# A hybrid layer on one core: fewer idle turns in a reordered opening, a context bank emptied by two copies, one weight and some row scalings moved back

## The chip, the core and the metric

The kernel runs on one core of a Trainium2 chip. A core has five engines that run side by side, each with its own queue of instructions in a fixed order: TensorE (PE in the profile: matrix products, its weight loads PEld), VectorE (DVE), ScalarE (ACT), GpSimd (POOL) and SyncE (SP), which here only issues the transfers from memory. They wait for each other by semaphores. Data live in memory (HBM), in SBUF (128 partitions) and in PSUM, whose banks of 128 x 512 floats take the results of TensorE. The metric is the device time of one execution in microseconds (us), lower is better.

## The reference

One layer of a diffusion backbone, for 1024 latent tokens on a 64-wide grid and 256 context tokens, with 1024 channels, in fp32. Cut to what matters:

```python
sh1, sc1, g1, sh2, sc2, g2 = jnp.split(c_silu @ w_ada[l] + b_ada[l], 6, axis=-1)
hx = _modulate(_rmsnorm(x, norm1_g[l]), sh1, sc1)      # h * (1 + scale) + shift
hc = _modulate(_rmsnorm(ctx, norm1_g[l]), csh1, csc1)
(xq, xk, xv, xrq, xrk, xrv, xrg, xga, xgb) = jnp.split(hx @ w_in[l], IN_OFFSETS, axis=-1)
...
o_na = _na_latent(...)      # neighbourhood attention, 8 heads of 64, plus all context keys
o_ret_x, _, _ = _bi_retention(...)   # 4 heads, keys of 128, values of 256, chunks of 128
o_ret = _ret_output(o_ret_x, xrg)
x = x + g1 * _merge(o_na, o_ret, xga, xgb, w_proj_na[l], w_proj_ret[l], w_out[l])
hx2 = _modulate(_rmsnorm(x, norm2_g[l]), sh2, sc2)
x = x + g2 * _conv_ffn(hx2, w_up[l], conv_w[l], conv_b[l], w_down[l])
...
return _rmsnorm(x, final_norm_g)
```

`_merge` multiplies the attention's output by `w_proj_na` (`w_pna` in the kernel) and the retention's by `w_proj_ret`, weighs each with a sigmoid gate and projects the sum by `w_out`. The first retention states come from the context tokens.

## The kernel before

Each fp32 operand is split into a rounded high part (a cast on ScalarE, line 89) and the remainder (a subtraction on VectorE, line 90). A product is then three TensorE products, high x high, high x low, low x high (`mm3`, lines 113 to 115; 124 to 126 when it is called through other helpers). Tokens come in tiles of 128 (`tb` 0 to 7 latent, 8 and 9 context), channels in eight blocks of 128 (`kb`).

The work runs in stages: the opening to about 92 us, attention to about 370, retention to about 700, then the attention's projection `pn` with its gates, the retention's projection and the output projection to about 1130, the up-projection to 1500, the down-projection to the end. Outside two hand-ordered blocks a scheduler sets each engine's order from estimated costs; instructions that are marked `late` may be put back.

*The opening* (from line 652) is ordered by hand: the lines of that block are the order on each engine. `load_x` and `load_ag` load token tiles and pieces of the modulation weight on SP; `load_f` loads the first attention weight. `square_x` (ScalarE), `rstd_x` (GpSimd), `scale_x` (VectorE) normalise a tile; `transp` turns its blocks on TensorE into PSUM (line 207). `ag_mm` (283) multiplies a piece of the modulation weight by the conditioning columns, `ag_ev`, `ag_tr` (293) and `ag_fin` make per-channel scale and shift of it, and `mod_h`, `mod_v`, `mod_l` make the high part, the full value and the low part of the modulated block. `evac_t` moves a turned block out of PSUM first. `first_mm(half, kb)` is the first attention pair's projection: nine products per block; `next_mm` the second pair's. `ctx_h`, `ctx_v`, `ctx_l` and `ctx_mm` do the same for the context tokens. `turn_idle` (197) lets TensorE transpose the identity for nothing; here 83 times.

*Retention.* `front(i)` projects one token tile of a head to queries, keys and values in one PSUM bank. For a context tile (`i < NCB`) three readers follow: the cast of the values (1138), the subtraction for their low part (1139), the copy of the keys `r0` (1143).

*Attention's projection.* After retention eight tiles `onr` of the attention's output are loaded and turned into banks `tpn` (1371; the pool `g` holds six banks), and split into `ona` (1373 on ScalarE, 1374 on VectorE). `hx_sums(k)` makes four sums of gate operands: GpSimd adds high and low parts into four buffers `b` (1354, from the pool `r` of ten, which also holds the `onr` tiles), VectorE combines them (1357) in four operations. `wpn` are the first two weights of the projection `pn`.

*The end of the down-projection.* For the last column half of token rows 4 to 7, VectorE forms a row part, GpSimd multiplies it by the gate (1972) and adds the residual (1973), ScalarE squares it (1923), and `early_part` (1927, 1928, GpSimd) scales it by the final gain.

Of the kernel before, what the change touches and what calls it, by code (L numbers as in the profile page):

```python
# [8 lines left out]
F32 = mybir.dt.float32  # L9
# [31 lines left out]
def tile_hybrid_layer(ctx, tc: tile.TileContext, io, dbg=None):  # L41
# [610 lines left out]
    with tc.manual_schedule():  # L652
        make_sel()
        load_x(0)
        square_x(0)
        load_x(3)
        load_x(2)
        load_cc()
        rstd_x(0, 1)
        load_x(1)  # L660
        square_x(3)
        scale_x(0)
        load_ag(0, 0)
        transp(0, (3,), ("c0",), idle=34)
        transp(0, (6,), ("c1",))
        load_ag(0, 1)
        silu_cc()
        load_cols()
        square_x(2)
        ag_mm(0, 0, idle=24)  # L670
        rstd_x(3, 1)
        load_ag(1, 0)
        transp(0, (7,), ("tp",))
        square_x(1)
        ag_mm(0, 1)
        transp(0, (0,), ("c1",), idle=3)
        load_ag(1, 1)
        transp(0, (5,), ("c1",))
        scale_x(3)
        transp(3, (6,), ("c1",))  # L680
        load_f(0, 0)
        rstd_x(2, 1)
        transp(3, (0,), ("c1",))
        scale_x(2)
        transp(0, (4,), ("c0",))
        rstd_x(1, 1)
        ag_ev(0, "act")
        transp(2, (3,), ("c0",))
        transp(3, (5,), ("c1",), idle=4)
        ag_tr(0)  # L690
        load_ag(2, 0)
        scale_x(1)
        load_ag(2, 1)
        load_f(0, 1)
        transp(2, (0,), ("c1",))
        transp(3, (3,), ("c0",))
        transp(2, (7,), ("tp",))
        one_plus()
        transp(1, (0,), ("c1",))
        transp(1, (6,), ("c1",))  # L700
        ag_mm(1, 0, idle=5)
        transp(1, (5,), ("c1",))
        ag_mm(1, 1)
        transp(0, (1,), ("c0",))
        load_ag(4, 0)
        transp(2, (4,), ("c0",))
        ag_fin(0)
        transp(1, (7,), ("tp",))
        mod_h(True, 0, 0)
        ag_ev(1, "act")  # L710
        load_f(0, 2)
        transp(2, (1,), ("c0",))
        transp(0, (2,), ("c1",))
        transp(1, (3,), ("c0",))
        load_x(5)
        transp(3, (1,), ("c0",))
        transp(2, (6,), ("c1",))
        mod_v(True, 0, 0)
        load_x(4)
        load_x(6)  # L720
        transp(3, (4,), ("c0",))
        transp(3, (7,), ("tp",))
        transp(2, (2,), ("c1",))
        mod_l(True, 0, 0)
        transp(1, (1,), ("c0",), idle=4)
        split_hi(0, 0)
        evac_t(True, 0, 3, "vec")
        ag_tr(1)
        ag_mm(2, 0, idle=5)
        load_x(7)  # L730
        evac_t(True, 0, 7, "act")
        ag_fin(1)
        mod_v(True, 0, 1)
        mod_h(True, 0, 1)
        ag_mm(2, 1)
        transp(1, (4,), ("c0",))
        transp(3, (2,), ("c1",))
        transp(2, (5,), ("c1",))
        split_lo(0, 0)
        ag_ev(2, "act")  # L740
        evac_t(True, 0, 4, "vec")
        load_ag(3, 0)
        transp(1, (2,), ("c1",), idle=4)
        split_hi(0, 1)
        ag_tr(2)
        split_hi(0, 2)
        ag_mm(4, 0)
        load_ag(3, 1)
        split_lo(0, 1)
        ag_fin(2)  # L750
        load_ag(4, 1)
        split_lo(0, 2)
        mod_l(True, 0, 1)
        load_ag(4, 2)
        mod_h(True, 0, 2)
        load_ag(4, 3)
        evac_t(True, 0, 6, "vec")
        mod_v(True, 0, 2)
        square_x(5)
        first_mm(0, 0)  # L760
        rstd_x(5, 1)
        mod_l(True, 0, 2)
        square_x(4)
        rstd_x(4, 1)
        square_x(6)
        scale_x(4)
        load_ex()
        first_mm(0, 1)
        scale_x(5)
        load_ag(5, 0)  # L770
        rstd_x(6, 1)
        scale_x(6)
        first_mm(0, 2)
        transp(4, (3,), ("c1",))
        ag_mm(3, 0)
        square_x(7)
        load_x(8)
        transp(4, (2,), ("c1",))
        load_x(9)
        rstd_x(7, 1)  # L780
        transp(5, (2,), ("c1",))
        transp(4, (0,), ("c1",))
        scale_x(7)
        transp(6, (3,), ("c1",))
        next_load(0)
        ag_mm(3, 1)
        transp(6, (2,), ("c1",))
        transp(6, (0,), ("c1",))
        evac_t(True, 0, 5, "act")
        transp(7, (2,), ("c1",))  # L790
        load_ag(5, 1)
        transp(7, (0,), ("c1",))
        transp(5, (3,), ("c1",))
        transp(7, (3,), ("c1",))
        ag_ev(3, "vec")
        transp(5, (0,), ("c1",))
        ag_tr(3)
        ag_mm(4, 1)
        transp(4, (5,), ("c1",))
        transp(4, (7,), ("c1",))  # L800
        transp(7, (5,), ("c1",))
        transp(6, (7,), ("c1",))
        evac_t(True, 1, 2, "vec")
        transp(6, (5,), ("c1",))
        transp(4, (4,), ("tp",))
        ag_fin(3)
        transp(5, (7,), ("c1",))
        transp(5, (5,), ("c1",))
        evac_t(True, 1, 0, "act")
        ag_mm(4, 2)  # L810
        transp(7, (4,), ("tp",))
        mod_h(True, 1, 0)
        ag_mm(4, 3)
        transp(4, (6,), ("c1",))
        mod_h(True, 0, 3)
        transp(5, (4,), ("tp",))
        transp(5, (6,), ("c1",))
        load_f(1, 0)
        mod_v(True, 1, 2)
        transp(6, (6,), ("c1",))  # L820
        load_f(1, 2)
        transp(6, (4,), ("tp",))
        transp(7, (7,), ("c1",))
        mod_v(True, 0, 3)
        mod_l(True, 0, 3)
        mod_v(True, 1, 0)
        ag_ev(4, "vec")
        evac_t(True, 1, 5, "act")
        transp(7, (6,), ("c1",))
        mod_h(True, 1, 2)  # L830
        first_mm(0, 3)
        transp(4, (1,), ("tp",))
        evac_t(True, 1, 3, "act")
        mod_v(True, 1, 3)
        transp(6, (1,), ("tp",))
        ag_tr(4)
        mod_l(True, 1, 0)
        evac_t(True, 1, 6, "vec")
        ag_fin(4)
        evac_t(True, 1, 7, "act")  # L840
        mod_v(True, 0, 4)
        transp(5, (1,), ("tp",))
        mod_l(True, 1, 2)
        evac_t(True, 1, 4, "act")
        transp(7, (1,), ("tp",))
        first_mm(1, 0)
        square_x(8)
        mod_v(True, 1, 1)
        mod_h(True, 1, 3)
        square_x(9)  # L850
        mod_h(True, 0, 4)
        load_ag(5, 2)
        first_mm(1, 2)
        mod_h(True, 1, 1)
        rstd_x(9, 1)
        mod_l(True, 0, 4)
        ag_mm(5, 0)
        mod_h(True, 1, 4)
        ag_mm(5, 1)
        ag_mm(5, 2)  # L860
        load_ag(5, 3)
        split_hi(1, 0)
        ag_mm(5, 3)
        mod_l(True, 1, 1)
        mod_h(True, 0, 5)
        scale_x(9)
        load_f(1, 1)
        mod_v(True, 1, 4)
        rstd_x(8, 1)
        first_mm(1, 1)  # L870
        mod_l(True, 1, 4)
        ag_ev(5, "act")
        split_lo(1, 0)
        mod_h(True, 1, 5)
        ag_tr(5)
        split_hi(1, 2)
        next_load(1)
        mod_l(True, 1, 3)
        scale_x(8)
        split_lo(1, 2)  # L880
        transp(8, (4,), ("tp",))
        split_hi(1, 1)
        mod_v(True, 1, 5)
        mod_l(True, 1, 5)
        ag_fin(5)
        first_mm(1, 3)
        split_lo(1, 1)
        transp(8, (2,), ("tp",))
        transp(9, (3,), ("tp",))
        transp(9, (5,), ("tp",))  # L890
        transp(9, (4,), ("tp",))
        mod_v(True, 0, 7)
        mod_h(True, 1, 7)
        mod_v(True, 0, 6)
        transp(8, (3,), ("tp",))
        ctx_h(3)
        first_mm(1, 4)
        mod_h(True, 1, 6)
        next_hi(0)
        mod_v(True, 1, 6)  # L900
        mod_h(True, 0, 6)
        transp(9, (2,), ("tp",))
        transp(8, (5,), ("tp",))
        ctx_v(3)
        mod_l(True, 1, 6)
        mod_v(True, 0, 5)
        load_bc()
        ctx_v(2)
        first_mm(0, 4)
        transp(8, (6,), ("tp",))  # L910
        mod_l(True, 0, 6)
        first_mm(1, 6)
        transp(8, (0,), ("tp",))
        ctx_h(2)
        ctx_h(5)
        mod_h(True, 0, 7)
        ctx_l(2)
        first_mm(1, 5)
        ctx_v(4)
        first_mm(0, 6)  # L920
        transp(9, (0,), ("tp",))
        ctx_l(3)
        ctx_h(4)
        ctx_v(5)
        mod_l(True, 0, 5)
        transp(9, (6,), ("tp",))
        ctx_h(6)
        ctx_l(4)
        mod_v(True, 1, 7)
        mod_l(True, 0, 7)  # L930
        first_mm(0, 5)
        ctx_v(6)
        ctx_h(0)
        ctx_l(6)
        transp(9, (1,), ("tp",))
        transp(8, (1,), ("tp",))
        ctx_v(1)
        next_lo(0)
        first_mm(0, 7)
        transp(9, (7,), ("tp",))  # L940
        ctx_h(1)
        mod_l(True, 1, 7)
        ctx_l(5)
        transp(8, (7,), ("tp",))
        first_mm(1, 7)
        ctx_v(0)
        ctx_l(1)
        ctx_l(0)
        ctx_v(7)
        ctx_h(7)  # L950
        ctx_l(7)
        s0.release()
# [18 lines left out]
        next_hi(1)  # L971
        ev_hi(1, 1, 0)
        next_lo(1)
        ev_hi(2, 1, 0)
        ev_hi(0, 1, 1)
        ev_lo(0, 1, 1)
# [1142 lines left out]
```

## Time and profile before

| | us |
|---|---|
| median of 3 runs (lowest, highest) | 1734.16 (1733.9, 1735.04) |
| the profiled execution | 1735.01 |
| its span, first to last instruction | 1733.2 |
| TensorE busy | 1717.1 (99%) |
| VectorE, ScalarE, GpSimd busy | 1222.2, 839.6, 540.4 |
| mean granted TensorE clock | 0.998 |

The page of the profile gives busy time by engine, the chain of work that ended last, and groups of instructions by line. A row of the timeline is: start, length of the group, engine, line, operation, output<-inputs, shapes, count, and in brackets the idle time before it with what ended it. A row of the windows is: stretch, its length, then busy time and count for PE, PEld, DVE, ACT and POOL, the granted clock, the busy share of the transfer engines and GB/s. Products overlap, so a group's length runs past the start of the next.

### The profile page before, as it was taken

Reading aid. Unit: us, or ns where it says so; the run is one execution under the profiler, and the core shown is the slowest. Engines: PE = TensorE matmul, PEld = TensorE weight load, DVE = VectorE, ACT = ScalarE, POOL = GpSimd, SP = SyncE. Lnnn points to the kernel's source line nnn. Section 1 sums busy time; section 2 is a strip of 40 time slices with the busy share of each in tenths; the row PEclk is TensorE's granted clock in tenths of the full one; section 3 lists DMA queues with packets and bytes.
Section 4 is the critical chain, followed back from the end, with each engine's and each line's share of the span. In section 5 each row is a group of like instructions: output and inputs, shape, how many; then the busy total and the mean of one; then the engine's idle time right before and its main releaser. Section 6 shows DMA issues by size and latency. Waiting matters only on the chain.

```text
span 1733.2 us, 25367 instructions
## 1 busy us (share of the span) xinstructions
PE 1717.1 (99%) x8552; PEld 1435.8 (83%) x8552; DVE 1222.2 (71%) x2461; ACT 839.6 (48%) x1796; POOL 540.4 (31%) x706
## 2 busy tenths in 40 slices
PE   9999999999999999999999999999999999999997
PEld 7788888888888888888888888788788888888886
DVE  5778787665676766855555657867888889856756
ACT  6566666563453434543444333644444444545444
POOL 2100000002334343512223121012667667311444
PEclk9999999999999999999999999999999999999999
DMA  9344455532231223588975656768666776998744
GB/s 378 95 138 143 141 158 160 151 118 64 68 101 37 77 46 109 180 273 256 277 241 201 217 184 181 272 216 230 172 165 179 196 192 168 261 313 294 242 153 175
DMA packets 142002, 313.04 MB, mean 181 GB/s; under 512 B 19152, under 2 KB 32112, under 8 KB 135664
## 3 DMA queue, kind: packets, MB, share of 16 engines
q1 hardware_dynamic: 117536, 230.40, 38.6%
q0 software_dynamic: 12032, 70.27, 18.1%
q10 hardware_dynamic: 12304, 10.75, 1.8%
q8 instruction: 67, 1.10, 0.2%
q14 instruction: 63, 0.52, 0.1%
HBM read 250.78 MB, written 121.91 MB: 215 GB/s over the span
## 4 chain that ended last, share of the span: by engine, by line
PE 81%; issue 5%; DMA 5%; DVE 5%; POOL 2%; ACT 2%; SPq 0%; POOLq 0%; ACTq 0%; DVEq 0%
PE u L1379 28%; PE mm L126 4%; PE mm L124 4%; PE mm L125 4%; PE mm L115 4%; PE mm L114 4%; PE mm L113 4%; PE y L1379 2%; PE R L516 2%; DMA ur<-d_a 2%; PE pr L114 2%; PE pr L113 2%; PE pr L115 2%; PE ptp L498 2%; PE om L125 1%
## 5 line engine op out<-in xcount | busy, mean ns | idle before, releaser
L1379 PE MATMUL u<-T,wc 128*128 128x512 f32 x960 | 225.3, 390 | 0.7 <-ACT pu L1413 0.5
L1379 PEld LDWEIGHTS u<-T,wc 128*128 128x128 f32 x960 | 179.4, 188 | 40.9 <-ACT pu L1413 3.7
L1379 PE MATMUL y<-wc,ahl 128*128 128x512 f32 x924 | 210.1, 389 | 0.4 <-DVE wc L90 0.4
L1379 PEld LDWEIGHTS y<-wc,ahl 128*128 128x128 f32 x924 | 173.3, 188 | 36.8 <-DVE wc L90 0.8
L90 DVE TENSOR_TENSOR wc<-ur,wc 128x512 fp32r<-128x512 f32 x161 | 119.2, 743 | 62.6 <-ACT wc L89 60.8
L89 ACT CAST wc<-ur 128x512 fp32r<-128x512 f32 x161 | 99.7, 621 | 117.7 <-PE u L1379 74.1
L114 PE MATMUL mm<-low,wc 128*128 128x512 f32 (+1 forms) x312 | 118.9, 381 | 0.0
L1379 PE MATMUL u<-h2a,wc 128*128 128x512 f32 x480 | 113.1, 390 | 0.4 <-DVE pu L1422 0.4
L113 PE MATMUL mm<-hx,wc 128*128 128x512 f32 x264 | 107.4, 407 | 0.3 <-ACT hc L227 0.3
L1379 PEld LDWEIGHTS u<-h2a,wc 128*128 128x128 f32 x480 | 89.7, 188 | 20.5 <-issue 1.5
L115 PE MATMUL mm<-hx,wc 128*128 128x512 f32 x264 | 105.3, 399 | 0.0
L1379 PE MATMUL u<-hxT,wc 128*128 128x512 f32 x384 | 89.6, 389 | 0.0
L587 POOL COPY pad<-pu 128x1 f32<-128x1 f32 x54 | 36.6, 678 | 163.2 <-DVE pu L1416 120.9
L587 POOL COPY pad<-st 128x1 f32<-128x1 f32 x32 | 5.9, 185 | 257.7 <-DVE st L490 257.7
L1379 PEld LDWEIGHTS u<-hxT,wc 128*128 128x128 f32 x384 | 72.1, 188 | 14.9
L89 ACT CAST wc<-raw 128x512 fp32r<-128x512 f32 x86 | 53.1, 621 | 43.6 <-PE pr L115 9.2
L126 PE MATMUL mm<-wc,low 128*128 128x512 f32 (+1 forms) x180 | 68.9, 383 | 0.0
L89 ACT CAST wc<-s 128x512 fp32r<-128x512 f32 x56 | 34.8, 622 | 70.3 <-PE u L1379 70.3
L90 DVE TENSOR_TENSOR wc<-raw,wc 128x512 fp32r<-128x512 f32 x86 | 61.0, 713 | 9.5 <-ACT wc L89 8.8
L114 PEld LDWEIGHTS mm<-low,wc 128*128 128x128 f32 x312 | 59.0, 189 | 7.0
L1379 PE MATMUL u<-hx,wc 128*128 128x512 f32 x192 | 61.9, 390 | 0.0
L90 DVE TENSOR_TENSOR ahl<-ur,ahl 128x512 fp32r<-128x512 f32 x66 | 52.3, 800 | 11.8 <-ACT ahl L89 11.7
(412 smaller groups left out, 4731.3 us busy)
## 6 DMA issues: line engine op xcount, KB each, us to landing
d_a<-at SPq DMA_DIRECT2D x77, 256.0 KB, 6.1
ur<-d_a SPq DMA_DIRECT2D x77, 256.0 KB, 5.3
ur<-in_w_up SPq DMA_DIRECT2D x74, 256.0 KB, 5.9
d_w<-in_w_down POOLq DMA_DIRECT2D x66, 256.0 KB, 7.3
aw<-in_w_ada SPq DMA_DIRECT2D x32, 512.0 KB, 3.6
d_a<-d_a POOLq DMA_DIRECT2D x44, 256.0 KB, 7.4
ur<-d_w SPq DMA_DIRECT2D x44, 256.0 KB, 3.8
d_s<-in_w_up POOLq DMA_DIRECT2D x36, 256.0 KB, 6.1
```

The lines of the kernel that those rows point to most:

```text
L89: act.copy(hi, src)
L90: (lo_eng or vec).tensor_tensor(lo, src, hi.bitcast(F32), ALU.subtract)
L113: pe.matmul(out, wh, xh, start=k == 0, stop=False)
L114: pe.matmul(out, wh, xl, start=False, stop=False)
L115: pe.matmul(out, wl, xh, start=False, stop=k == n - 1)
L124: pe.matmul(out, ah, bh, start=first, stop=False)
L125: pe.matmul(out, ah, bl, start=False, stop=False)
L126: pe.matmul(out, al, bh, start=False, stop=last)
L498: pe.transpose(tp[:, c], self.Pm[h][:, c * P : (c + 1) * P], ident)
L516: pe.matmul(R[:, h], self.pair.V[:, g, h].rearrange("p a b -> p (a b)"), self.PT[h][:, c].rearrange("p a b -> p (a b)"), start=c == 0, sto ...
L587: late(pool.tensor_copy(tick, src))
L1379: pe.matmul(out, a, b, start=first and n == 0, stop=last and n == 2, skip_group_check=True)
```

## The change

Five things change.

1. In the opening the idle turns go from 83 in eight groups to 51 in two, 29 before the first transpose and 22 before the first modulation product. The order of almost all other steps of the block is new too. On SP, `f(0,1)` comes ahead of `ag(1,0)`, `x5` and `x4` later than `ag(4,0)`, and `lg` and `ex` (decay constants) come last. On TensorE the transposes `(2,6)` and `(3,6)` stand behind `first_mm(0,2)`, and `next_mm(0,0)` comes first of its four.
2. For the two context tiles of the first retention head, a VectorE copy takes the values from the bank to an SBUF tile `r1` and a ScalarE copy takes the keys; cast and subtraction of the values then read `r1`.
3. The second weight `wpn` is loaded and split behind the transposes of `onr` in the code.
4. In the last quarter of the down-projection the four `early_part` calls stand behind the loop and no longer inside it.
5. All else, and what is computed, is as before.

The diff, cut to its core:

```diff
     with tc.manual_schedule():
-        make_sel()
         load_x(0)
+        load_x(3)
         square_x(0)
...
+        transp(0, (5,), ("c1",), idle=29)
...
-        transp(0, (3,), ("c0",), idle=34)
-        transp(0, (6,), ("c1",))
...
-        ag_mm(0, 0, idle=24)
...
-        transp(0, (0,), ("c1",), idle=3)
...
+        ag_mm(0, 0, idle=22)
         load_f(0, 0)
         rstd_x(2, 1)
+        load_f(0, 1)
+        load_cols()
+        load_ag(1, 0)
...
-        transp(3, (5,), ("c1",), idle=4)
...
-        ag_mm(1, 0, idle=5)
...
+        ag_mm(1, 0)
...
-        transp(1, (1,), ("c0",), idle=4)
...
-        ag_mm(2, 0, idle=5)
...
+        ag_mm(2, 0)
         ag_mm(2, 1)
...
-        transp(1, (2,), ("c1",), idle=4)
...
+        first_mm(0, 0)
+        load_ag(3, 0)
...
+        first_mm(0, 1)
         rstd_x(5, 1)
+        transp(2, (6,), ("c1",))
         mod_l(True, 0, 2)
...
+        first_mm(0, 2)
+        transp(3, (6,), ("c1",))
...
-        load_ex()
...
+        load_ex()
+        first_mm(1, 4)
...
@@ front @@
             vtag = f"c{i}" if i < NCB else tb
             self.v[i] = v = rt.tile([P, 2, DV], F32R, tag=f"v{vtag}", bufs=1, name="v")
-            act.copy(v[:, 0], m[:, 256:512])
-            vec.tensor_tensor(v[:, 1], m[:, 256:512], v[:, 0].bitcast(F32), ALU.subtract)
             r0 = rt.tile([P, 2, 2, 2, 32], F32, tag="r0", bufs=2, name="r0")
+            r1 = rt.tile([P, 2, 2, 2, 32], F32, tag="r1", bufs=2, name="r1")
             self.r0[i] = r0f = r0.rearrange("p q a t i -> p q (a t i)")
+            vm = m[:, 256:512]
+            if i < NCB and self.h == 0:
+                vm = r1.rearrange("p q a t i -> p (q a t i)")
+                vec.tensor_copy(vm, m[:, 256:512])
+                act.copy(r0f[:, 1], m[:, P : 2 * P])
+            act.copy(v[:, 0], vm)
+            vec.tensor_tensor(v[:, 1], vm, v[:, 0].bitcast(F32), ALU.subtract)
             if i < NCB:
-                act.copy(r0f[:, 1], m[:, P : 2 * P])
+                if self.h:
+                    act.copy(r0f[:, 1], m[:, P : 2 * P])
                 return
-            r1 = rt.tile([P, 2, 2, 2, 32], F32, tag="r1", bufs=2, name="r1")
@@ behind retention @@
-    wpn = [wload(io["w_pna"][db, 0]) for db in range(2)]
+    wpn = [wload(io["w_pna"][0, 0])]
...
         act.copy(dst[0], tp)
         vec.tensor_tensor(dst[1], tp, dst[0].bitcast(F32), ALU.subtract)
+    wpn.append(wload(io["w_pna"][1, 0]))
@@ down-projection @@
         pool.tensor_tensor(z, z, x, ALU.add)
         square(QB + b, 1, x)
+    for b in range(QB):
         early_part(QB + b, 1)
```

What stands on the engines. First TensorE between the first modulation products and the first `first_mm` (L124): `c` and `tp` are PSUM tiles, L197 are idle turns, L207 transposes, L283 `ag_mm`, L293 `ag_tr`. Before, a piece with two groups of turns:

```order
L207 MATMUL c_349<-ident,x 128x128
L197 MATMUL c_335<-ident 128x128 x4
L207 MATMUL c_335<-ident,x 128x128
L293 MATMUL tp<-sel_157,arow 128x2 x2
L197 MATMUL tp<-ident 128x128 x5
L283 MATMUL tp<-x,ccol 32x256 x8
L207 MATMUL c_293<-ident,x 128x128
L207 MATMUL c_349<-ident,x 128x128
L207 MATMUL c_283<-ident,x 128x128
L197 MATMUL c_349<-ident 128x128 x4
L207 MATMUL c_349<-ident,x 128x128
L293 MATMUL tp<-sel_157,arow 128x2 x2
```

Now, up to the same product:

```order
L207 MATMUL c_332<-ident,x 128x128
L207 MATMUL c_227<-ident,x 128x128
L293 MATMUL tp<-sel_157,arow 128x2 x2
L207 MATMUL c_179<-ident,x 128x128
L207 MATMUL c_227<-ident,x 128x128
L207 MATMUL c_221<-ident,x 128x128
L207 MATMUL c_332<-ident,x 128x128
L283 MATMUL tp<-x,ccol 32x256 x12
L293 MATMUL tp<-sel_157,arow 128x2 x2
L124 MATMUL c_396<-hx_124,wc 128x8x8x8
```

The turns between are gone, and the three modulation products of `ag(2,0)`, `ag(2,1)` and `ag(4,0)` follow each other.

Next VectorE where retention ends: `wc` is a weight tile, `ona` the low part of the attention's output, `b` the sums, `pnt` the first use of a `pn` bank. Before:

```order
L90 TENSOR_TENSOR wc<-raw,wc 128x512 x2
L1374 TENSOR_TENSOR ona_8563<-tpn,ona_8562 128x4x128 x8
L1357 TENSOR_TENSOR b<-b 128x512
L1513 TENSOR_TENSOR pnt<-pn,sgt 128x512
L1357 TENSOR_TENSOR b<-b 128x512
L90 TENSOR_TENSOR hxT_8557<-b,hxT_8556 128x512
L1357 TENSOR_TENSOR b<-b 128x512
L1513 TENSOR_TENSOR pnt<-pn,sgt 128x512
L1357 TENSOR_TENSOR b<-b 128x512
```

Now (line 1361 is the former 1357, 1378 the former 1374):

```order
L1361 TENSOR_TENSOR b_8614<-b_8614,b_8612 128x512
L90 TENSOR_TENSOR wc_8828<-raw_8826,wc_8828 128x512
L1361 TENSOR_TENSOR b_8612<-b_8612,b_8616 128x512
L90 TENSOR_TENSOR wc_8873<-raw_8871,wc_8873 128x512
L1361 TENSOR_TENSOR b_8616<-b_8616,b_8614 128x512
L1361 TENSOR_TENSOR b_8618<-b_8618,b_8616 128x512
L1378 TENSOR_TENSOR ona1_8534<-tpn_8551,ona0_8533 128x4x128
```

The four operations of `hx_sums(0)` moved ahead of the eight subtractions `ona`. GpSimd makes the sums in the order `b_8612`, `b_8614`, `b_8616`, `b_8618`; the second VectorE operation on them reads the third. The loads and casts of the two weights stand where they stood.

Last GpSimd near the end of the down-projection: L1972 and L1973 multiply and add a row part, L1927 and L1928 are `early_part`. Before, from the third row's multiplication:

```order
L1972 TENSOR_TENSOR x2_16858<-x2_16858,gate2_15529 128x512
L1973 TENSOR_TENSOR x2_16849<-x2_16849,xr_16847 128x512
L1927 TENSOR_SCALAR ssf_15531<-ssf_15531 128x1
L1928 TENSOR_TENSOR x2_16840<-x2_16840,fg_15527 128x512
L1973 TENSOR_TENSOR x2_16858<-x2_16858,xr_16856 128x512
L1972 TENSOR_TENSOR x2_16867<-x2_16867,gate2_15529 128x512
L1927 TENSOR_SCALAR ssf_15531<-ssf_15531 128x1
L1928 TENSOR_TENSOR x2_16849<-x2_16849,fg_15527 128x512
L1927 TENSOR_SCALAR ssf_15531<-ssf_15531 128x1
L1928 TENSOR_TENSOR x2_16858<-x2_16858,fg_15527 128x512
L1973 TENSOR_TENSOR x2_16867<-x2_16867,xr_16865 128x512
```

Now:

```order
L1977 TENSOR_TENSOR x2_16830<-x2_16830,gate2_15505 128x512
L1978 TENSOR_TENSOR x2_16823<-x2_16823,xr_16821 128x512
L1978 TENSOR_TENSOR x2_16830<-x2_16830,xr_16828 128x512
L1977 TENSOR_TENSOR x2_16837<-x2_16837,gate2_15505 128x512
L1932 TENSOR_SCALAR ssf_15507<-ssf_15507 128x1
L1933 TENSOR_TENSOR x2_16816<-x2_16816,fg_15503 128x512
L1978 TENSOR_TENSOR x2_16837<-x2_16837,xr_16835 128x512
```

One pair of `early_part` is left ahead of the fourth row's add; the second and third row's pairs follow it.

More of the change, by code (lines that the diff above doesn't have):

```diff
@@ L690, in tile_hybrid_layer @@
[L690 to L699, printed above, removed]
+        load_ag(1, 1)
+        transp(3, (5,), ("c1",))
+        one_plus()
+        transp(3, (7,), ("tp",))
+        load_ag(2, 0)
+        load_ag(2, 1)
+        transp(3, (0,), ("c0",))
+        ag_mm(0, 1)
+        ag_ev(0, "act")
+        transp(1, (0,), ("c0",))
@@ L765, in tile_hybrid_layer @@
+        ag_mm(3, 0)
+        load_ag(4, 1)
         square_x(6)
-        scale_x(4)
-        load_ex()
-        first_mm(0, 1)
+        square_x(7)
         scale_x(5)
-        load_ag(5, 0)
         rstd_x(6, 1)
         scale_x(6)
-        first_mm(0, 2)
-        transp(4, (3,), ("c1",))
[L775 to L782, printed above, removed]
-        scale_x(7)
@@ L799, in tile_hybrid_layer @@
+        transp(4, (4,), ("tp",))
+        transp(7, (6,), ("c1",))
+        ag_mm(4, 1)
+        ag_mm(4, 2)
+        load_x(9)
+        mod_v(True, 1, 2)
+        ag_mm(4, 3)
+        load_f(1, 1)
         transp(4, (5,), ("c1",))
+        load_ag(5, 2)
+        mod_h(True, 1, 3)
         transp(4, (7,), ("c1",))
+        mod_h(True, 1, 2)
+        load_f(1, 2)
+        transp(5, (6,), ("c1",))
+        mod_h(True, 0, 3)
+        load_x(8)
+        mod_v(True, 1, 3)
+        transp(5, (7,), ("c1",))
@@ L831, in tile_hybrid_layer @@
[L831 to L847, printed above, removed]
-        mod_v(True, 1, 1)
@@ L906, in tile_hybrid_layer @@
[L906 to L909, printed above, removed]
+        mod_l(True, 1, 1)
+        next_load(0)
+        mod_v(True, 1, 4)
+        split_lo(1, 1)
+        mod_v(True, 1, 5)
+        ag_mm(5, 3)
+        mod_l(True, 0, 4)
+        rstd_x(8, 1)
+        scale_x(8)
+        first_mm(1, 1)
+        transp(8, (2,), ("tp",))
+        ag_ev(5, "vec")
+        first_mm(1, 3)
+        transp(9, (3,), ("tp",))
+        split_lo(1, 2)
+        transp(9, (2,), ("tp",))
```

392 lines of the change are left out of this document (192 added, 200 removed).

## The prediction

> **What bounds the kernel now.** I read the busy shares first, then the chain that ended last, then the windows and the timeline of the four places that the change touches.
>
> ```profile
> span 1733.2 us, 25367 instructions
> PE 1717.1 (99%) x8552; PEld 1435.8 (83%) x8552; DVE 1222.2 (71%) x2461; ACT 839.6 (48%) x1796; POOL 540.4 (31%) x706
> PE 81%; issue 5%; DMA 5%; DVE 5%; POOL 2%; ACT 2%; SPq 0%; POOLq 0%; ACTq 0%; DVEq 0%
> ```
>
> TensorE is busy for 99% of the span and holds 81% of the chain. So only what lets PE start earlier, or makes it stand, counts, and as PE has almost no idle time anywhere to absorb a lag, a lag made at 705 us is still there at 1733 us. The sum below is therefore one of shifts of PE's queue, place by place. It is made against the profiled execution, 1735.01 us (the span and 1.8 us around it), which is 0.85 us above the median 1734.16; I put the shifts on the median.
>
> **The opening, up to the first product.** PE's timeline (start, length of the group, count) and windows (the second column is PE busy, the last three are granted clock, DMA share, GB/s):
>
> ```profile
> 1.37 6.72 PE L197 MATMUL c<-ident 128*128 128x128 f32 x34 [1.37 <-POOL ident masks.py:199]
> 8.14 2.78 PE L197 MATMUL tp<-ident 128*128 128x128 f32 x24
> 22.29 0.64 PE L283 MATMUL tp<-x,ccol 128*32 128x256 f32 x8
> 22.86 0.50 PE L124 MATMUL c<-hx,wc 128*128 128x512 f32 x1
> ...
> 7.10:22.86 15.76, 15.71 (x159) 12.12 (x157) 7.89 (x16) 7.11 (x14) 2.32 (x5) 1.00 1.03 405
> 45.21:69.95 24.74, 23.65 (x115) 18.56 (x111) 18.83 (x38) 10.42 (x19) 4.77 (x4) 1.00 0.04 11
> ```
>
> A turn takes 2.78 / 24 = 0.116 us, some 0.111 from start to start. The change keeps 51 of 83 turns, all ahead of the first modulation product; the six groups between the second modulation product and the first `first_mm` (3, 4, 5, 4, 5, 4: 25 turns, 2.8 us of PE), go, and two transposes (0.22 us) move behind the first product at 22.86. One end is therefore −3.0, if the turns were pure delay. They were not: the queue of loads is full (share 1.03). Up to `ag(4,0)`, which the last group of products before 22.86 reads, the same bytes are queued in both orders, so it lands no earlier; `f(0,1)`, 256 KB, moves ahead of `ag(1,0)` to `ag(2,1)` and makes these 256 KB / 405 GB/s = 0.65 us later. The other end is +0.65, if the turns only filled waits for loads. I take −1.0, a third of the first end, since at 22.29 the product of `ag(4,0)` began without a wait behind a turn and a transpose. The `load_x` and `load_ag` that come later on SP change places among themselves; the queue is done by 45 us (share 0.04 after); `lg` and `ex`, now last, are read on VectorE only after 45 us, beside products.
>
> **From the first product to the next.** 22.86 to 69.95 (the first product of the next pair) are 47.09 us. The groups of this stretch and two waits:
>
> ```profile
> L124 PE MATMUL c<-hx,wc 128*128 128x512 f32 x48 | 19.8, 413 | 0.0
> L283 PE MATMUL tp<-x,ccol 128*32 128x256 f32 x76 | 5.5, 387 | 0.0
> L207 PE MATMUL tp<-ident,x 128*128 128x128 f32 x24 | 5.1, 280 | 0.8 <-ACT hc L227 0.7
> L207 PE MATMUL c<-ident,x 128*128 128x128 f32 x24 | 4.1, 284 | 0.0
> L293 PE MATMUL tp<-sel,arow 128*128 128x4 f32 x8 | 1.0, 232 | 0.0
> ...
> 56.02 0.33 PE L207 MATMUL tp<-ident,x 128*128 128x128 f32 x1 [0.74 <-ACT hc L227]
> 69.95 0.50 PE L113 MATMUL mm<-hx,wc 128*128 128x512 f32 x1 [0.26 <-ACT hc L227]
> ```
>
> The first row has two more of its kind. Back to back, a 512-column product starts 0.227 us after the last, one of `ag_mm` 0.071, a transpose 0.111: 144 × 0.227 + 76 × 0.071 + 48 × 0.111 + 12 × 0.1 (the last row and four of its kind) = 44.6 us. So 2.5 us are lost in switches and waits. The new order groups the products (three blocks of nine run before the first new transpose) and takes both transposes that wait for a context bank to another place. Some 0.9 us of switches must stay, so −1.6. Ends: −2.5, and +1.0, if the dense context work on ScalarE and VectorE makes one more pair of waits like the two shown (0.74 + 0.26).
>
> **First retention context.** The bank holds three readers, one after another:
>
> ```profile
> 378.94 0.37 ACT L1138 CAST v<-mm 128x256 fp32r<-128x256 f32 x1 [2.09 <-PE mm L126]
> 379.35 0.42 DVE L1139 TENSOR_TENSOR v<-mm,v 128x256 fp32r<-128x256 f32 x1 [1.61 <-ACT v L1138]
> 380.19 0.50 PE L124 MATMUL mm<-wc,hx 128*128 128x512 f32 x1 [0.63 <-ACT r L1143]
> ```
>
> The third is ScalarE's copy `r`, which releases PE's product. Now one copy on each engine leaves the bank, and the cast and the subtraction read SBUF. Of the three steps one, about 0.4, goes: −0.4; ends −0.63, the whole wait, and +0.3 if the added VectorE copies hold back `kz`.
>
> **The row scalings moved back.** On GpSimd the fourth add came behind three pairs that scale earlier rows; PE then waited 0.38 us for a weight whose cast stood behind that row's square on ScalarE:
>
> ```profile
> 1679.12 1.29 POOL L1973 TENSOR_TENSOR x<-x,xr 128x512 f32<-128x512 f32 x1
> 1680.44 0.63 ACT L1923 ACTIVATE xr<-x 128x512 f32<-128x512 f32 x1 [4.89 <-POOL x L1973]
> 1683.42 6.87 PE L1379 MATMUL y<-wc,ahl 128*128 128x512 f32 x29 [0.38 <-DVE wc L90]
> ```
>
> Now one pair stands ahead of that add; the other two, each with a multiplication as long as the add's 1.29, follow it, so it is some 3 us earlier and the wait goes with its switch: −0.5, ends −0.5 and 0. The scalings themselves end before the next rows need GpSimd.
>
> **The moved weight.** The load and cast of `w_pna[1]` stay where they were on SP and ScalarE. What moves is VectorE's queue: the four subtractions and additions of `hx_sums(0)` now stand ahead of the eight subtractions `ona`. Here it was:
>
> ```profile
> 699.39 0.68 DVE L90 TENSOR_TENSOR wc<-raw,wc 128x512 fp32r<-128x512 f32 x1
> 703.70 4.86 DVE L1374 TENSOR_TENSOR ona<-tpn,ona 128x512 fp32r<-128x512 f32 x8
> 708.48 0.72 DVE L1357 TENSOR_TENSOR b<-b 128x512 f32<-128x512 f32 x1
> 710.83 1.78 DVE L90 TENSOR_TENSOR hxT<-b,hxT 128x512 fp32r<-128x512 f32 x1
> 712.53 1.77 DVE L1357 TENSOR_TENSOR b<-b 128x512 f32<-128x512 f32 x1
> ...
> 701.94 11.81 POOL L1354 TENSOR_TENSOR b<-hx,low 128x512 f32<-128x512 f32 x8 [2.63 <-PE tpn L1371]
> ...
> 701.26 2.78 PE L1371 MATMUL tpn<-ident,onr 128*128 128x128 f32 x24
> 704.43 1.25 PE L1371 MATMUL tpn<-ident,onr 128*128 128x128 f32 x8 [0.38 <-DVE ona L1374]
> 706.22 0.50 PE L114 MATMUL pn<-ona,wc 128*128 128x512 f32 x1
> ```
>
> GpSimd's third addition `b` waits for a buffer that PE's transposes release, so it starts at 701.94 and, at 1.3 us (11.81 / 8 = 1.48 with VectorE beside it), ends at 703.2. The second VectorE operation of `hx_sums` needs it, and behind it stand the split of the weight, two more operations of `hx_sums`, and only then `ona`. GpSimd meanwhile runs the other seven additions of that group back to back. An operation of VectorE with both inputs in SBUF takes 0.68 to 0.72 alone and 1.77 to 1.78 in the midst of such additions. At the latter (it is the nearer row: the same instructions, the same additions) 4 × 1.7 = 6.8 us, and `ona` starts at 710.0, not 703.70: +6.3. Queued behind it: PE's last eight transposes need the banks of the first two `ona`, so PE stands from about 704 to 710.5, and the first `pn` product with `ona`'s low part needs four of them (4 × 0.61), so it starts at 712.5, not 706.22: +6.3. At 0.7 each, the lower end, `ona` starts at 706.0: +2.3. The upper end is a full addition (1.3) ahead of each 0.7: 8.0 in all, +7.5.
>
> [...]
>
> **The clock in that gap.**
>
> ```profile
> 6.00:7.00 1.00, 1.00 (x7) 1.00 (x6) 0.75 (x1) 0.72 (x2) 0.27 (x2) 1.00 1.02 364
> 7.00:8.00 1.00, 1.00 (x10) 1.00 (x9) 0.32 (x1) 0.00 (x0) 0.56 (x2) 1.00 1.01 362
> 1719.82 4.47 PE L1379 MATMUL y<-wc,ahl 128*128 128x512 f32 x19
> 1727.00:1728.00 1.00, 0.00 (x0) 0.00 (x0) 0.40 (x1) 0.58 (x2) 0.55 (x1) 0.72 0.00 0
> 1728.00:1729.00 1.00, 0.00 (x0) 0.00 (x0) 0.35 (x1) 0.32 (x1) 0.00 (x0) 0.50 1.00 369
> ```
>
> PE's last product ends at 1724.29; the granted clock is 0.72 on average over 1727 to 1728 and 0.50 after, so it fell at 1727.44, 3.2 us after PE stopped. At the start it went the other way: the pace of turns rose (7, then 10 in a microsecond) at about 7.1 us, 5.7 us after the first (the clock column already reads 1.00 there, so the pace is the better witness). A stand of 6.5 us is longer than 3.2, so I expect half clock when PE resumes at 710.5. If it lasts 5.7 us, PE works in some 4.6 of them and loses 2.3; if 3.2, it loses 0.7 at least. I take +1.7, ends 0 and +2.9.
>
> [...]
>
> **Sum.** −1.0 − 1.6 − 0.4 − 0.5 + 6.3 + 1.7 = +4.5: 1734.16 + 4.5 = 1738.7.
>
> **Rivals.**
> - *Contention, clock kept* (chance 0.20): the idle time at 704 is cut by PE's early products, or the clock falls but recovers before the products at 712.5. −3.5 + 6.3 = +2.8: 1737.0.
> - *Little contention* (0.15): the four operations fall between GpSimd's additions, as the one at 708.48 did; +2.3, PE stands for 2.5 us only, below 3.2, and the clock stays. −3.5 + 2.3 = −1.2: 1733.0.
> - *Faster* (0.06): the third addition no longer waits for PE (701.94), so that `hx_sums` is through VectorE before the transposes; the place costs nothing and −3.5 is left: 1730.7. It decides if `ona` starts before 704.3. Against it: the buffers of the eight loaded tiles and two sums fill the pool of ten, so the third must wait.
> - *The opening gives nothing* (0.12): without the turns PE waits for loads or for the context banks instead, and the rest stays: −0.9 + 6.3 + 1.7 = +7.1: 1741.3.
> - That the scheduler undoes the move of the weight on the chip cannot be; each engine runs its queue in the order that is written.
>
> **How the numbers follow.** The forecast has 0.42, 0.05 is left for anything else. 0.2%, or 3.5 us, is about what a measurement of this kernel can tell from no change. Below −3.5: 0.06 (the fourth case and its neighbours). Above +3.5: most of the forecast's 0.42 (its bounds of +6.3 and +1.7 put some of it under), the 0.12 of the last rival, a little of the first: 0.53. Within: 0.41. The range goes from the third case less its spread, 1732.4, to the last one, 1741.6; it leaves out the faster case, the rest, and the tails. The forecast's own range is 1737 to 1740.5.
>
> **What the profile after should show.** First product at about 21.8 us; the first product of the next pair at 67 to 67.6. At the bank of the context, PE's wait near 377 below 0.3. On VectorE four operations of 1.6 to 1.8 between the third `b` of GpSimd and the first `ona`, which is 6 us behind the last transposes of the first 24; PE with a gap of 5 to 7 us there, and a granted clock below 1 in the window behind it. Near 1680 no wait of PE for `wc`. I am wrong if that gap is below 3 us, if the clock column stays at 1.00 behind it, or if the lead at the next pair's first product is under 1 us.

## The result, and the profile after

The changed kernel takes 1738.77 us (median of 20, from 1734.93 to 1742.92); the kernel before took 1734.28 us in the same comparison (1733.23 to 1735.75). The ratio is 1.0024, 95% interval 1.0017 to 1.0031: slower by 4.5 us at the medians (the ratio weighs all executions and gives 4.2), and with a spread of 8.0 us where before it was 2.5. The profiled execution has a span of 1736.6 us.

The page after, and the windows around the place of the moved weight (columns as before: stretch, length, busy time and count of PE, PEld, DVE, ACT and POOL, granted clock, DMA share, GB/s):

```profile
span 1736.6 us, 25303 instructions
PE 1713.0 (99%) x8520; PEld 1434.7 (83%) x8520; DVE 1224.8 (71%) x2460; ACT 841.0 (48%) x1797; POOL 542.2 (31%) x706
PE 92%; DVE 3%; DMA 2%; ACT 1%; issue 1%; POOL 0%; SPq 0%; POOLq 0%; ACTq 0%
...
700.00:702.00 2.00, 0.33 (x3) 0.09 (x1) 2.00 (x2) 1.77 (x4) 2.00 (x2) 1.00 0.38 143
702.00:703.00 1.00, 0.00 (x0) 0.00 (x0) 1.00 (x2) 0.00 (x0) 1.00 (x2) 0.86 0.04 16
703.00:712.00 9.00, 5.02 (x16) 4.37 (x17) 7.98 (x10) 3.60 (x6) 6.93 (x5) 0.50 0.13 31
712.00:713.00 1.00, 1.00 (x4) 0.72 (x4) 0.00 (x0) 1.00 (x4) 0.00 (x0) 0.52 0.00 0
713.00:716.00 3.00, 3.00 (x15) 2.47 (x14) 2.28 (x4) 1.07 (x3) 0.91 (x1) 1.00 0.25 89
```

TensorE is still busy for 99%, so the time is again a sum of shifts in its queue. The clock is half from 702.7 us (a mean of 0.86 in that microsecond) to 713.0.

The timelines of the four places after:

```profile
20.16 0.64 PE L283 MATMUL tp<-x,ccol 128*32 128x256 f32 x8 [1.60 <-DMA x<-in_w_ada1g]
21.19 0.48 PE L124 MATMUL c<-hx,wc 128*128 128x512 f32 x1
67.40 0.39 PE L113 MATMUL mm<-hx,wc 128*128 128x512 f32 x1
376.48 0.50 PE L124 MATMUL mm<-wc,hx 128*128 128x512 f32 x1 [0.16 <-ACT r L1143]
697.54 2.78 PE L1375 MATMUL tpn<-ident,onr 128*128 128x128 f32 x24
706.98 1.94 PE L1375 MATMUL tpn<-ident,onr 128*128 128x128 f32 x8 [6.66 <-issue]
708.57 0.78 PE L113 MATMUL pn<-ona,wc 128*128 128x512 f32 x1
709.14 0.63 PE L114 MATMUL pn<-ona,wc 128*128 128x512 f32 x1
713.22 0.40 PE L115 MATMUL pn<-ona,wc 128*128 128x512 f32 x1
1675.75 14.44 PE L1384 MATMUL y<-wc,ahl 128*128 128x512 f32 x63
...
698.22 9.18 POOL L1358 TENSOR_TENSOR b<-hx,low 128x512 f32<-128x512 f32 x6 [2.62 <-PE tpn L1375]
...
699.53 1.75 DVE L1361 TENSOR_TENSOR b<-b 128x512 f32<-128x512 f32 x1 [2.56 <-POOL b L1358]
701.20 1.75 DVE L90 TENSOR_TENSOR wc<-raw,wc 128x512 fp32r<-128x512 f32 x1
702.87 3.41 DVE L1361 TENSOR_TENSOR b<-b 128x512 f32<-128x512 f32 x2
706.20 4.86 DVE L1378 TENSOR_TENSOR ona<-tpn,ona 128x512 fp32r<-128x512 f32 x8
```

The first and the twelfth `pn` product of the kernel before, which the prediction does not show:

```profile
705.71 0.47 PE L113 MATMUL pn<-ona,wc 128*128 128x512 f32 x1
708.62 0.39 PE L115 MATMUL pn<-ona,wc 128*128 128x512 f32 x1
```

Read as shifts against the rows before: the next pair's first product comes at 67.40 (69.95 before, −2.55), the product behind the first context's bank at 376.48 (380.19, −3.71), the transposes of the attention's output at 697.54 (701.26, −3.72). Then TensorE stands for 6.66 us, VectorE runs its four operations of about 1.7 us ahead of `ona`, and the first `pn` product comes at 708.57 (705.71, +2.86), the one with the low part at 709.14 (706.22, +2.92). The products behind it are 0.43 us apart until the clock is back; at the twelfth, 713.22 (708.62), the shift is +4.60 and stays there. The run of 63 products near 1680 us has no wait for `wc` in it any more.

### The profile page after: what moved, and what is told of

Its sections match the earlier page's. It is cut to its first block, busy times and chain, and to the rows that moved or that the text cites. A ratio compares the mean times of both kernels' runs of the same rounds, so it can differ in the third digit from the quotient of the medians.

```text
span 1736.6 us, 25303 instructions
## 1 busy us (share of the span) xinstructions
PE 1713.0 (99%) x8520; PEld 1434.7 (83%) x8520; DVE 1224.8 (71%) x2460; ACT 841.0 (48%) x1797; POOL 542.2 (31%) x706
## 4 chain that ended last, share of the span: by engine, by line
PE 92%; DVE 3%; DMA 2%; ACT 1%; issue 1%; POOL 0%; SPq 0%; POOLq 0%; ACTq 0%
PE u L1384 30%; PE y L1384 12%; PE mm L126 4%; PE mm L124 4%; PE mm L125 4%; PE mm L115 4%; PE mm L114 4%; PE mm L113 4%; PE R L516 2%; PE pr L115 2%; PE pr L113 2%; PE pr L114 2%; PE ptp L498 2%; PE om L126 1%; PE om L124 1%; PE om L125 1%
## 5 line engine op out<-in xcount | busy, mean ns | idle before, releaser
L89 ACT CAST wc<-wr 128x512 fp32r<-128x512 f32 x56 | 34.8, 621 | 59.3 <-PE u L1384 50.0
```

What stands on the lines that cost most here:

```text
L89: act.copy(hi, src)
```

## The experiments

**The weight alone, and all but the weight.** The first kernel is the one before with only

```diff
-    wpn = [wload(io["w_pna"][db, 0]) for db in range(2)]
+    wpn = [wload(io["w_pna"][0, 0])]
...
         vec.tensor_tensor(dst[1], tp, dst[0].bitcast(F32), ALU.subtract)
+    wpn.append(wload(io["w_pna"][1, 0]))
```

> The kernel before with the second weight's load moved behind the transposes and nothing else. My theory: the same gap of 6 to 7 us on PE and the same fall of the clock: 1734.3 + 6.6 + 1.6 = 1742.5. Rival (the gap needs the early arrival): 1734 to 1736.

Measured: 1742.65 us against 1734.62, ratio 1.0044 (1.0031 to 1.0058), +8.0 us at the medians. The gap is the same without any early arrival:

```profile
701.13 2.78 PE L1371 MATMUL tpn<-ident,onr 128*128 128x128 f32 x24
710.57 1.94 PE L1371 MATMUL tpn<-ident,onr 128*128 128x128 f32 x8 [6.66 <-issue]
```

The reverse, the changed kernel with these lines taken back:

> The changed kernel with both projection weights loaded and split where they were before; all else of the change stays. My theory (the moved weight put hx_sums ahead of ona on VectorE, which cost 6.6 us of waiting and about 1.6 us of clock): ona starts right behind the weight's split, PE waits under 1 us there, granted clock 1.00 from 700 to 716 us, and the leads of the opening, the bank and the end are left: 1734.3 - 3.7 - 0.7 = about 1730.0. Rival (the loss is not tied to the order on VectorE but to the earlier arrival at that place, with transfers or buffers not ready): the gap stays, 1738.

Measured: 1731.91 us against 1734.62, ratio 0.9986 (0.9977 to 0.9995), −2.7 us. The last transposes wait 0.38 us as before and the clock stays at 1.00 there, so the place is cleared of its cost:

```profile
703.91 1.25 PE L1375 MATMUL tpn<-ident,onr 128*128 128x128 f32 x8 [0.38 <-DVE ona L1378]
```

But I expected a gain of about 4.4 us, so 1.7 are missing, and the spread is 6.3 us. This is taken up below under the opening.

**Contention or slow operations.** In the changed kernel the later additions leave GpSimd:

```diff
-            late(pool.tensor_tensor(t, hxp(0, kb, c0, 512).bitcast(F32), hxp(1, kb, c0, 512).bitcast(F32), ALU.add))
+            late((vec if k else pool).tensor_tensor(t, hxp(0, kb, c0, 512).bitcast(F32), hxp(1, kb, c0, 512).bitcast(F32), ALU.add))
```

> The changed kernel with the first additions of hx_sums(1) to hx_sums(3) moved from GpSimd to VectorE, later in its queue, so that GpSimd is idle while VectorE runs the four operations and the weight's split ahead of ona. Theory (contention: VectorE's operations on two SBUF inputs wait for GpSimd's additions): these operations take 0.7 us and not 1.75, ona starts some 2.8 us and not 6 us behind the third addition, PE stands for about 2.7 us, the clock stays at 1.00; about 1738.8 - 3.9 - 1.6 = 1733.3, plus whatever the twelve additions cost on VectorE later (0 to 4 us). Rival (the operations are slow of themselves or by ScalarE's reads): they take 1.7 us all the same and the gap stays at 6.6 us.

Measured: 1734.3 us against 1734.62, ratio 0.9996 (0.9988 to 1.0005). VectorE and GpSimd at the place:

```profile
701.12 1.74 DVE L1361 TENSOR_TENSOR b<-b 128x512 f32<-128x512 f32 x1 [2.56 <-POOL b L1358]
702.79 0.68 DVE L90 TENSOR_TENSOR wc<-raw,wc 128x512 fp32r<-128x512 f32 x1
703.39 1.46 DVE L1361 TENSOR_TENSOR b<-b 128x512 f32<-128x512 f32 x2
...
699.81 2.50 POOL L1358 TENSOR_TENSOR b<-hx,low 128x512 f32<-128x512 f32 x2 [2.61 <-PE tpn L1375]
...
705.56 1.94 PE L1375 MATMUL tpn<-ident,onr 128*128 128x128 f32 x8 [3.64 <-issue]
```

The first operation still runs beside GpSimd's fourth addition (699.81 + 2.50 = 702.31) and takes 1.74; the three behind it, with GpSimd idle, take 0.68 and 1.46 for two. So the same instructions cost 1.75 beside GpSimd and about 0.7 without, and the additions on GpSimd made 3.0 of the 6.66 us of the gap (6.66 − 3.64). The other part is the order itself: the wait for the third addition and four operations at 0.7. The subtractions `ona`, which read a bank of PSUM, took nearly the same in both: 0.61 each beside the additions in the kernel before (4.86 for eight), 0.63 here with GpSimd idle (1.88 for the first three). What I missed: a stand of 3.64 us was enough for the clock to fall here too, for 3.4 us (a mean of 0.56 from 705 to 706 us, 0.50 from 706 to 708, 0.74 from 708 to 709).

**The clock.** TensorE is kept busy in the gap of the changed kernel by turns that nobody reads; two more lines keep the splits of `hx_sums(0)` in program order:

```diff
         tp = pg.tile([P, NPAIR, P], F32, tag="g", bufs=6, name="tpn")
+        if n == 5:
+            turn_idle(tp[:, 0], 56)
```

> The changed kernel with 56 idle turns of TensorE (6.2 us) ahead of the sixth tile's transposes, where TensorE would stand, so that it stays busy; the splits of hx_sums(0) are kept in program order so that VectorE's order up to the eighth ona stays. Theory A (the clock falls because PE stands, and turns count as work): granted clock 1.00 from 700 to 716, products behind the gap at 0.227 us, the wait for ona stays, so 1738.8 - 1.6 = 1737.2. [...]

Measured: 1735.75 us against 1734.62, ratio 1.0009 (1.0 to 1.0018); the changed kernel itself stands at 1.0024.

```profile
698.67 2.35 PE L1381 MATMUL tpn<-ident,onr 128*128 128x128 f32 x20
700.85 6.28 PE L197 MATMUL tpn<-ident 128*128 128x128 f32 x56
708.16 1.23 PE L1381 MATMUL tpn<-ident,onr 128*128 128x128 f32 x8 [0.60 <-PE tpn L1381]
709.41 0.47 PE L113 MATMUL pn<-ona,wc 128*128 128x512 f32 x1
709.91 0.50 PE L114 MATMUL pn<-ona,wc 128*128 128x512 f32 x1
...
700.00:712.00 12.00, 11.35 (x88) 10.10 (x87) 11.25 (x12) 8.48 (x15) 10.69 (x8) 1.00 0.29 96
```

The wait for `ona` stays, since turns do not bring it, but the clock is 1.00 throughout, where in the changed kernel it was 0.61 on average from 700 to 712 us. Theory A holds: with turns in the gap the clock did not fall. In the profiled executions this was worth 2.0 us: here the place costs 6.3 us (from 2.59 ahead at the transposes, 698.67 for 701.26, to 3.70 behind at the first `pn` product, 709.41 for 705.71, and no more after it), in the changed kernel 8.3 (from −3.72 to +4.60). The medians differ by 3.0 us, but the opening's spread is in both.

**The opening alone.** The kernel before with the whole new block, nothing else (the diff is the first part of the change's own):

> The kernel before with the new opening and nothing else. Theory: the new order starts the next pair's first product 2.5 us earlier (67.4 against 69.95) when the clock holds, and only 0.7 to 1.0 us earlier when the clock falls for some 3.5 us behind the wait for the load of ag(4,0) near 19 us, as two profiled executions showed; so 1734.6 - 2.6 to - 1.0, a median near 1732.7 with a spread of 5 us or more. Rival (the fall of the clock is a matter of those two executions alone): 1731.5 and a spread like before's, 2.5 us.

Measured: 1734.15 us against 1734.18, ratio 1.0 (0.9992 to 1.0009), single times from 1730.36 to 1738.14. The profiled execution, the slowest of the eleven, was one in which the clock fell, and it fell twice. PE's products in the opening, a later wait with the clock behind it and, from the kernel with both weights early, the clock in another such opening:

```profile
17.64 1.07 PE L283 MATMUL tp<-x,ccol 128*32 128x256 f32 x16
20.22 0.64 PE L283 MATMUL tp<-x,ccol 128*32 128x256 f32 x8 [1.51 <-DVE low L215]
22.64 0.63 PE L124 MATMUL c<-hx,wc 128*128 128x512 f32 x1
23.92 0.63 PE L124 MATMUL c<-hx,wc 128*128 128x512 f32 x1
68.52 0.39 PE L113 MATMUL mm<-hx,wc 128*128 128x512 f32 x1
146.32 0.78 PE L498 MATMUL ptp<-ident,P 128*128 128x128 f32 x4 [1.99 <-ACT P L487]
...
147.00:148.00 1.00, 1.00 (x9) 0.84 (x8) 0.16 (x1) 1.00 (x5) 0.00 (x0) 0.80 0.93 332
```

```profile
22.00:23.00 1.00, 1.00 (x5) 0.87 (x6) 1.00 (x2) 0.82 (x2) 0.00 (x0) 0.86 1.02 406
24.00:26.00 2.00, 2.00 (x6) 1.60 (x5) 0.79 (x2) 1.97 (x4) 1.05 (x4) 0.50 1.03 412
26.00:27.00 1.00, 1.00 (x5) 0.79 (x5) 0.59 (x1) 0.97 (x3) 0.64 (x2) 0.94 1.02 406
```

Three products take 1.28 us in this opening (22.64 to 23.92) and not 0.69. TensorE had waited 1.4 to 1.5 us for the load of `ag(4,0)`, where the turns used to stand. (The bracket of the second row names VectorE's copy `low`, which ended at 20.1 us; the load, issued at 11.9, took 8.2 to land, so it came at the same time.)

What the fall costs can be read from the first `first_mm` product to the next pair's first. With a fall it took 47.3 us (21.25 to 68.52 here, 21.60 to 68.91 in the contention kernel, 21.95 to 69.24 with both weights early), without one 46.2 (21.19 to 67.40 in the changed kernel, 21.50 to 67.72 with turns in the gap), and in the kernel before 47.1. So a fall in the opening costs 1.1 us; the rest of the differences at the next pair is when the load landed.

That is not the whole loss. At 68.52 this execution was still 1.4 us ahead of the kernel before, and it ended 3.2 us behind (spans of 1736.4 and 1733.2 us). It lost 3.0 us near 146 us, where TensorE waited 1.99 us for ScalarE's `P`, a tile of attention weights (0.39 before), and the clock fell again, for 3.41 us. It lost 1.7 more near 1105 us, in a wait for a tile `h2l`, the low part of the up-projection's input. The wait for `P` was 0.3 to 0.5 us in the five profiled executions with the old order of the opening and 0.3 to 2.0 in the seven with the new; why it varies is open.

The mean clock of each execution, which is on record, tells how often it fell. The clock is half at the end of the program too, behind the last product, for 3.1 to 6.9 us in the twelve profiled executions. A mean of 0.999 is at most 5.2 us at half, which leaves no room for a fall of 3.4 beside the end's 3.1; 0.997 is at least 8.7, more than the end alone makes. Here the four executions at 0.999 took 1730.36 to 1732.85 us, the four at 0.998 took 1733.0 to 1735.09, the three at 0.997 took 1734.15 to 1738.14. So the new opening is worth about 2.2 us in the executions without a fall (1732.0 on average) and nothing over all. With both weights early it is the same: 1731.0 on average at 0.999, 1733.7 at 0.997. The kernel before, with its turns, is at 0.998 or 0.999 in all 79 executions of the three comparisons that list it, and no profiled execution with the old order had a fall in the opening.

**The middle turns alone.** The kernel before without its 25 turns of the middle, order as it was:

```diff
-        ag_mm(1, 0, idle=5)
+        ag_mm(1, 0)
```

(and likewise the five other groups of 3 to 5.)

> The kernel before without the 25 idle turns of the middle (34 and 24 stay), order unchanged. Theory A (the turns filled waits for loads): the first product at 22.0 to 22.9 us, so 0 to -0.9 us of gain while the clock holds, and +1.6 us in executions in which it falls; 1733.7 to 1736. Theory B (the turns were pure delay): the first product at 20 us and 1731.8.

Measured: 1732.85 us against 1734.18, ratio 0.9999 (0.999 to 1.0008). The first product was at 21.68 us, 1.2 us earlier than before, a little more than theory A gave. Seven times lie between 1731.86 and 1732.94 and four between 1735.4 and 1736.97, so the median is 1.3 us lower but the ratio, which weighs them all, is 1. The profiled execution (1732.67) is of the first group and held its clock. A fall of the clock does not make the second group: 1735.58 and 1735.65 have a mean clock of 0.999, which leaves no room for one. What does is open.

**Turns where TensorE waits for the load.** To the kernel with both weights early:

```diff
-        ag_mm(4, 0)
+        ag_mm(4, 0, idle=12)
```

> The kernel with both weights early and 12 idle turns (1.3 us) ahead of the products of ag(4,0), where TensorE otherwise waits 1.4 to 1.6 us for that load. Theory A (without turns the clock falls behind this wait in some executions): granted clock 1.00 from 16 to 28 us, products at 0.227 us, the next pair's first product at 67.4 to 67.8; median about 1730.5 and a narrower spread than the 6 us of the same kernel without these turns. Theory B (the turns do nothing for the clock): about 1731.9, and products at 0.43 us between 22 and 26 us in some executions.

Measured: 1729.44 us against 1734.18, ratio 0.9972 (0.9962 to 0.9982), times from 1727.81 to 1730.4. This is faster than the kernel before and the changed one by more than the intervals.

```profile
19.29 1.53 PE L197 MATMUL tp<-ident 128*128 128x128 f32 x12
20.75 0.64 PE L283 MATMUL tp<-x,ccol 128*32 128x256 f32 x8
21.79 0.48 PE L124 MATMUL c<-hx,wc 128*128 128x512 f32 x1
22.57 0.39 PE L124 MATMUL c<-hx,wc 128*128 128x512 f32 x1
23.26 0.39 PE L124 MATMUL c<-hx,wc 128*128 128x512 f32 x1
68.03 0.39 PE L113 MATMUL mm<-hx,wc 128*128 128x512 f32 x1
...
16.00:22.00 6.00, 6.00 (x64) 4.26 (x65) 4.01 (x9) 3.66 (x8) 0.00 (x0) 1.00 1.03 405
22.00:28.00 6.00, 6.00 (x28) 4.86 (x28) 4.17 (x8) 5.64 (x10) 2.75 (x6) 1.00 1.03 411
```

The load lands while the turns run, the products start at once, and three of them take 0.69 to 0.78 us. The spread goes from 6.3 to 2.6 us, no execution is at a mean clock of 0.997 any more, and against the kernel before in the same comparison the median is 4.7 us lower, where without these turns it was 2.7. The fall in the opening explains 1.1 of these 2.0 us at most. Between the two profiled executions 1.2 us are there at the next pair's first product (68.03 and 69.24); the other 3.2 of their 4.4 come later, at the waits for `P` and `h2l` and in the up-projection, and that the turns brought them is not shown.

The same 12 turns in the changed kernel as it is, weight moved:

> The changed kernel, weight moved as it is, with the 12 idle turns ahead of the products of ag(4,0). Theory (two falls of the clock are in the changed kernel: one behind the gap at 704 us in nearly every execution, one in the opening in some): the opening's fall goes, the other stays; the median 1738.8 - 1 to - 2 = 1737 to 1738, the spread 4 us and not 8. Rival (the opening's fall does not matter with the weight moved, or the gap alone makes the spread): 1738.8 and a spread of 8 us.

Measured: 1737.06 us against 1733.89, ratio 1.0019 (1.001 to 1.0028), times from 1734.61 to 1740.31: 1.7 us less at the median than the changed kernel's 1738.77, and a spread of 5.7 us. In its profiled execution the clock is 1.00 in the opening and half from 703.4 to 713.6. The profiled execution of the changed kernel had no fall in the opening either. But two of its twenty have a mean clock of 0.994, at least 19 us at half, more than the gap's 10.2 and the end's 6.9 make; so there was another fall in them, in the opening or behind it. The intervals of the two ratios overlap, so the size of this part is not sharp.

**The two small parts.** The kernel before with the context's copies alone:

> The kernel before with the two copies out of the first context banks and nothing else. Theory: TensorE's wait behind the bank goes from 0.63 to 0.16 us, a shift of -0.4 to -0.5 us that stays in TensorE's queue; in the time it can hardly be told, 1734.1. Rival (the added VectorE copies hold back kz and the states): the wait goes to a later product of dS and the shift is 0.

Measured: 1733.65 us against 1734.18, ratio 0.9997 (0.9987 to 1.0007). The wait shrank as expected, and no other took its place within the next products:

```profile
379.24 0.50 PE L124 MATMUL mm<-wc,hx 128*128 128x512 f32 x1 [0.16 <-ACT r L1145]
```

The kernel before with the row scalings alone:

> The kernel before with the four row scalings behind their loop and nothing else. Theory: the fourth add on GpSimd starts some 3 us earlier, TensorE no longer waits 0.4 us for the weight near 1683 us; a shift of -0.5 us, in the time 1734 to 1734.5. Rival (the last row's square or the scaling is then late for the end): the wait stays or another of the same size takes its place.

Measured: 1734.08 us against 1733.89, ratio 1.0001 (0.9991 to 1.0011). GpSimd's fourth add ran 4 us earlier (1675.13, was 1679.12) and the products near 1683 have no wait. By the same products of both traces TensorE's lead over the kernel before goes from 0.35 us in front of the place to 1.03 behind it; the 0.7 us are below what the time can tell.

## Why the prediction was right, and where it was not

The time came out at 1738.77 for a forecast of 1738.7. Step by step:

- *The moved weight* (+6.3 and +1.7 for the clock). Shown. Alone it cost 8.0 us (interval 5.4 to 10.1), the sum of the two terms, and in the profiled execution the place cost 8.3: 6.3 with the clock held by turns, and 2.0 for the clock. The gap was 6.66 us, with four operations of 1.70 us on average where I took 1.7; the upper end, 2.0 each, was an estimate, and none of the four took more than 1.75. The clock fell 2.4 us after TensorE stopped (3.2 estimated) and was half for 10.2 us, 6.0 of them behind TensorE's return (5.7 estimated).
- *The bank* (−0.4). Shown on the wait: 0.63 to 0.16. The shift is −0.5 in all seven kernels that have the two copies.
- *The row scalings* (−0.5). Shown on the wait: gone. The shift is −0.7 in all seven kernels that have them moved.
- *The opening up to the first product* (−1.0). It was −1.7 in the profiled execution. The wait for `ag(4,0)` that I expected to eat most of the turns was there, 1.6 us, but it ate less of them.
- *The opening from there on* (−1.6). It was −0.9 while the clock held (46.2 us for 47.1). The two errors of 0.7 cancel: the whole lead was 2.55 us, my −2.6, by luck. And here the step failed that left the clock out: with a fall the term is +0.2, and the lead at the next pair 0.7 to 1.4. I weighed the idle time of 6.5 us at 704 us for the clock and not the wait of 1.5 us at 19 us, which the turns had covered; I also held a stand under 3.2 us to be safe for the clock, and waits of 1.4 us were not. Over all executions the new opening alone was worth 0.0 us (interval −1.4 to +1.6). The fall in the opening is 1.1 us of that; in the profiled execution the greater part was the wait for `P` at 146 us with its own fall, at a place that the prediction does not name. The rival in which the opening gives nothing named waits and context banks as the reason; waits had a share in it, the clock it did not see.

So the hit is partly luck: +8.0 for the weight and an opening that gives little on average leave more than 4.5 (8.0 − 0.4 − 0.5 = +7.1, the price of that rival), while the kernel without the moved weight is 2.7 us faster than before, which would leave +5.3. The intervals of the single runs, 1.5 to 2.5 us each way, allow both, so the parts are not shown to add up to the whole.

What stays open: the second wait for an `h2l` tile, near 1105 us, varies from none to 1.8 us, and the short waits of TensorE in the up-projection, each a shift of about half a microsecond, from none to four, in kernels that are alike there. With the wait for `P` at 146 us they are part of every spread shown here; their cause is open.

## What to carry to other kernels

A load that is moved in the code can move something else: here the weight stayed and VectorE's sums went ahead of the operations that freed TensorE's banks, so compare the order on every engine before reading a diff by its words. Count what such a block costs at the price beside GpSimd's additions, not alone (1.75 us against 0.7 here, for operations with both inputs in SBUF; 0.61 and 0.63 for the subtractions `ona`). Idle turns of TensorE paid here where it would otherwise have stood for 1.4 to 1.6 us for a load (the ratio went from 0.9986 to 0.9972) and for 6.66 us in the gap (from 1.0024 to 1.0009). The 25 that stood in the middle of the old opening could go at no gain or loss that the ratio shows.

## What the runs showed of the hardware

The half-clock stretches had two lengths in the profiled executions, those at the end of the program aside. In the gap they lasted 10.24 us in three kernels (702.72 to 712.96, 706.24 to 716.48, 703.40 to 713.64, worked out from the mean clock of the microseconds at their ends), in the opening, near 146 us and in the shorter gap 3.40 to 3.42 us (22.72 to 26.12, 22.44 to 25.86, 21.30 to 24.72, 147.60 to 151.01, 705.12 to 708.52). (Seven executions of the changed kernel have a mean clock of 0.997, too high for 10.24 us and the end's 3.1, so their gap had less.)

The time from TensorE's stop to the fall was not one figure. In the gap it was 2.40 us in the changed kernel (700.32 to 702.72), 2.33 with the weight alone (703.91 to 706.24) and 3.20 with the additions off GpSimd (701.92 to 705.12); in the openings 2.59 (18.71 to 21.30, the opening alone) and 3.29 (19.43 to 22.72, both weights early); at the end of the program 3.15 in the kernel before (1724.29 to 1727.44) and 5.26 in the changed one (1728.28 to 1733.54).

The length of a wait alone does not tell whether the clock falls. It fell behind waits of 6.66 and 3.64 us in the gaps and 1.99 near 146 us, and behind 1.48 and 1.51 in the openings. In the changed kernel a wait of 1.60 in the opening and one of 1.69 near 1109 us, for a tile `h2l`, brought no fall. In the opening alone TensorE had resumed before the clock fell (products from 20.22, fall at 21.30). What decides is not shown by these runs.
